# Holding back the first store, longer load rows, and a closing barrier moved to GpSimd, in a 2x nearest-neighbour upsampling kernel

## The chip, the cores and the metric

The kernel runs on one core of a Trainium2 chip. The metric is the device time of one execution in microseconds (us), as the median of several runs. From one run to the next the time of one kernel moves by 0.1 to 0.7 us, and the effects discussed here are of that order on about 199 us. So the times are always set beside the kernel before from the same rounds on the same chip, and the trace, which resolves nanoseconds, is used to tell where the time lies. The span of a trace (first to last instruction) is about 1.8 us shorter than the reported time.

## The reference

```python
x: (16, 64, 64, 64) float32, scale_factor = 2
result: (16, 64, 128, 128) float32
result[:, :, i, j] = x[:, :, i // 2, j // 2]
```

Every input value is written four times: 16.78 MB are read and 67.11 MB written, 83.89 MB in all. There is no arithmetic.

## The kernel before

The input is seen as 65536 rows of 64 numbers. It is loaded in four DMAs of 4 MB, all issued at the start on SyncE's queue into the 128 partitions. The first three put 32 KB of consecutive data into each partition; the fourth is cut into four bands, so that a partition gets four pieces of 8 KB. VectorE expands 9/16 of each chunk and ScalarE the rest into one of two buffers, and a DMA on the same SyncE queue stores the buffer: eight stores of 4 MB (one row of 32 KB per partition), then four of 8 MB (64 KB per partition).

```python
M4 = R // (4 * P)                       # 128 input rows per partition and block
blocks = [(1, M4, 0), (1, M4, 2), (1, M4, 3), (4, M4 // 4, 1)]
... # cut
for n, (j, m, slot) in enumerate(blocks):
    first = n * P * M4
    xt = mem[:, slot * WB : (slot + 1) * WB].rearrange("p (j m w) -> p j m w", j=j, m=m)
    nc.sync.dma_start(
        out=xt.rearrange("p j m w -> p j (m w)"),
        in_=xf[first : first + P * M4, :].rearrange("(j p m) w -> p j (m w)", j=j, p=P),
    )
... # cut
def store(part, r0, k, at):
    xp, first, m = part
    kv = k * 9 // 16
    u = mem[:, at : at + k * s * W * s].rearrange("p (k a w b) -> p k a w b", k=k, a=s, w=W)
    nc.vector.tensor_copy(out=u[:, :kv], in_=expanded(xp[:, r0 : r0 + kv, :]))
    nc.scalar.copy(out=u[:, kv:], in_=expanded(xp[:, r0 + kv : r0 + k, :]))
    dst = of[first : first + P * m, :].rearrange("(p m) w -> p m w", p=P)
    nc.sync.dma_start(out=dst[:, r0 : r0 + k, :], in_=u)

small = [(q, r0) for n in (0, 3) for q in parts[n] for r0 in range(0, q[2], 32)]
large = [(q, r0) for n in (1, 2) for q in parts[n] for r0 in range(0, q[2], 64)]
for n, (q, r0) in enumerate(small):
    store(q, r0, 32, WX + n % 2 * (WU // 2))
for n, (q, r0) in enumerate(large):
    store(q, r0, 64, (0, WX)[n % 2])
```

At the end of the program SyncE waits for all DMAs, then all five engines meet at a barrier, GpSimd clears the semaphores, and they meet at a second barrier.

Of the kernel before, what the change touches and what calls it, by code (L numbers as in the profile page):

```python
# [1 line left out]

# [4 lines left out]



EARLY = 1  # L10


def begin_before_barrier(nc):



    blocks = nc.main_func.blocks
    main, body = blocks[0], blocks[1]
    sp = mybir.EngineType.SP
    loads = [i for i in body.instructions if i.engine == sp][:EARLY]  # L20
    for load in loads:
        assert isinstance(load, mybir.InstDMACopy), type(load)
        assert not (load.sync_info and load.sync_info.on_wait)
    names = [i.name for i in loads]
    body.instructions = [i for i in body.instructions if i.name not in names]
    kept = list(main.instructions)
    at = next(
        n
        for n, i in enumerate(kept)
        if i.engine == sp and isinstance(i, mybir.InstDrain)  # L30
    )
    kept[at:at] = loads
    main.instructions = kept


@with_exitstack
def kernel(
    ctx: ExitStack,
    tc: tile.TileContext,
    x: bass.AP,  # L40
    scale_factor: int,
    out: bass.AP,
):
    nc = tc.nc
    nc.at_finalize(begin_before_barrier)
    P = nc.NUM_PARTITIONS
    s = int(scale_factor)
    B, C, H, W = x.shape
    R = B * C * H
    fdt = x.dtype  # L50



    WX = R // P * W
    WU = 16384
    mem_pool = ctx.enter_context(tc.tile_pool(name="mem", bufs=1))
    mem = mem_pool.tile([P, WX + WU], fdt, name="mem")



    M4 = R // (4 * P)
    blocks = [(1, M4, 0), (1, M4, 2), (1, M4, 3), (4, M4 // 4, 1)]
    WB = M4 * W
    assert M4 * P * 4 == R and 2 * WB == WU

    xf = x.rearrange("b c h w -> (b c h) w")
    of = out.rearrange("b c (h hd) w -> (b c h) (hd w)", hd=s)

    parts = []
    for n, (j, m, slot) in enumerate(blocks):  # L70
        first = n * P * M4
        xt = mem[:, slot * WB : (slot + 1) * WB].rearrange(
            "p (j m w) -> p j m w", j=j, m=m
        )
        nc.sync.dma_start(
            out=xt.rearrange("p j m w -> p j (m w)"),
            in_=xf[first : first + P * M4, :].rearrange(
                "(j p m) w -> p j (m w)", j=j, p=P
            ),
        )  # L80
        parts.append([(xt[:, jj], first + jj * P * m, m) for jj in range(j)])

    def expanded(rows):
        return rows.unsqueeze(2).unsqueeze(4).to_broadcast(
            [P, rows.shape[1], s, W, s]
# [6 lines that stand above are left out]
        u = mem[:, at : at + k * s * W * s].rearrange(  # L92
            "p (k a w b) -> p k a w b", k=k, a=s, w=W
        )
        nc.vector.tensor_copy(out=u[:, :kv], in_=expanded(xp[:, r0 : r0 + kv, :]))  # L95
        nc.scalar.copy(out=u[:, kv:], in_=expanded(xp[:, r0 + kv : r0 + k, :]))  # L96
        dst = of[first : first + P * m, :].rearrange("(p m) w -> p m w", p=P)
        nc.sync.dma_start(out=dst[:, r0 : r0 + k, :], in_=u)



    small = [(q, r0) for n in (0, 3) for q in parts[n] for r0 in range(0, q[2], 32)]
    large = [(q, r0) for n in (1, 2) for q in parts[n] for r0 in range(0, q[2], 64)]
    for n, (q, r0) in enumerate(small):
        store(q, r0, 32, WX + n % 2 * (WU // 2))
    for n, (q, r0) in enumerate(large):
        store(q, r0, 64, (0, WX)[n % 2])


# [1 line left out]
_INS = ['x', 'scale_factor']  # L111
_OUTS = [((16, 64, 128, 128), 'float32')]

_NUMBERS = {'scale_factor': 2}


# [26 lines left out]
```

## Time and profile before

| | before |
|---|---|
| time, median of the first 3 runs | 199.46 us (199.43 to 199.73) |
| span of the trace | 197.71 us |
| VectorE, ScalarE busy | 20%, 26% |
| DMA queue busy, mean rate over the span | 98.9%, 424 GB/s |
| last load landed / first store landed / last store landed | 42.19 / 51.90 / 196.90 us |
| last landing to end of span | 0.81 us |

These lines are from the page of the kernel before. The DMA row gives the busy share of the DMA engines in tenths for 40 slices of the span. The queue line gives packets, MB, and the share of the 16 engines' time. The last three lines give DMA groups: count, KB each, and the median time from issue to landing.

```profile
span 197.7 us, 116 instructions
DMA  8999999999999999999999999999999999999994
q1 hardware_dynamic: 2688, 83.89, 98.9%
HBM read 16.78 MB, written 67.11 MB: 424 GB/s over the span
out_dram<-mem SPq DMA_DIRECT2D x8, 4096.0 KB, 16.1
mem<-in_x_dram SPq DMA_DIRECT2D x4, 4096.0 KB, 25.8
out_dram<-mem SPq DMA_DIRECT2D x4, 32.3
```

The DMA engines are busy 90% or more in every slice but the first and the last. A store takes 16.1 us from issue to landing only because it waits about 6.4 us behind its predecessor; the pace itself has to be read from successive landings. The chain of waits shows it. Its columns are start, duration and what it was; a DMA piece runs from issue to landing. The part from 64 to 120 us:

```profile
64.87 16.05 DMA out_dram<-mem
80.92 0.02 issue
80.94 0.02 ACTq L96
80.95 0.04 issue
81.00 3.19 ACT mem L96
84.18 0.02 issue
84.20 16.08 DMA out_dram<-mem
100.28 0.02 issue
...
103.56 16.09 DMA out_dram<-mem
```

From 64.87 to 84.20 the chain makes one round, in which the queue moves two stores: 19.33 us, or 9.67 us for 4 MB, which is 434 GB/s. The next round is 19.36 us.

The waits of SyncE (SPq), which issues the DMAs (two lines of five; what waited, for what: us in total, times, longest), show when the first store can go and where the end is spent:

```profile
SPq L98 <- DVE mem L95: 143.5, 11, 35.7
SPq L138 <- DMA out_dram<-mem: 31.8, 2, 19.3
```

SyncE never waits for a load before it issues a store; it waits for the copies, VectorE's above all, and at the end (L138 is the end of the program) for the last stores.

### The profile page before, as it was taken

How to read it: one execution, taken by the hardware profiler on the slowest of the kernel's cores; microseconds unless marked ns; L12 is line 12 of the kernel's file. 1: busy time of each engine (PE TensorE's matmuls, PEld its weight loads, DVE VectorE, ACT ScalarE, POOL GpSimd, SP SyncE). 2: the span in 40 equal slices, each digit the busy share in tenths (PEclk: the TensorE clock that was granted, in tenths of full speed). 3: DMA queues.
4: the chain of work that ended last, by engine and by line, in shares of the span. 5: the costliest groups of instructions: out<-in, count | busy, mean ns of one | idle time of the engine just before them, and what ended most of it. 6: DMA issues, size and time to landing. Idle time of an engine off the chain costs nothing.

```text
span 197.7 us, 116 instructions
## 1 busy us (share of the span) xinstructions
DVE 40.2 (20%) x12; ACT 51.3 (26%) x13; POOL 0.2 (0%) x4
## 2 busy tenths in 40 slices
DVE  0055000000405059505050007200810090000000
ACT  2057000000415150606069207400830092000000
POOL 0000000000000000000000000000000000000000
DMA  8999999999999999999999999999999999999994
GB/s 318 424 424 424 438 464 383 424 413 424 424 424 424 444 444 451 451 424 438 424 424 424 424 424 424 464 477 491 451 451 424 424 424 424 424 424 424 424 424 212
DMA packets 2688, 83.89 MB, mean 424 GB/s; under 512 B 256, under 2 KB 256, under 8 KB 256
## 3 DMA queue, kind: packets, MB, share of 16 engines
q1 hardware_dynamic: 2688, 83.89, 98.9%
HBM read 16.78 MB, written 67.11 MB: 424 GB/s over the span
## 4 chain that ended last, share of the span: by engine, by line
DMA 69%; ACT 14%; issue 0%; ACTq 0%
DMA out_dram<-mem 63%; ACT mem L96 14%; DMA mem<-in_x_dram 6%; ACTq L96 0%
## 5 line engine op out<-in xcount | busy, mean ns | idle before, releaser
L96 ACT COPY mem<-mem 128x3584 f32<-128x3584 f32 (+1 forms) x12 | 50.0, 4174 | 112.5 <-DMA out_dram<-mem 102.2
L95 DVE COPY mem<-mem 128x4608 f32<-128x4608 f32 (+1 forms) x12 | 40.2, 3359 | 123.1 <-DMA out_dram<-mem 110.8
L96 ACT ACT_TABLE_LOAD x1 | 1.3, 1283 | 0.8 <-PEq L124 0.8
L124 POOL MEMSET const-bfloat16-1.0<- 128x1 bf16 x1 | 0.1, 102 | 0.0
L124 POOL MEMSET const-uint8-127<- 128x1 uint8 x1 | 0.1, 102 | 0.0
L124 POOL MEMSET const-float32-0.0<- 128x1 f32 x1 | 0.1, 99 | 0.2 <-issue 0.2
L124 POOL MEMSET const-float32-1.0<- 128x1 f32 x1 | 0.1, 99 | 0.0
## 6 DMA issues: line engine op xcount, KB each, us to landing
out_dram<-mem SPq DMA_DIRECT2D x8, 4096.0 KB, 16.1
mem<-in_x_dram SPq DMA_DIRECT2D x4, 4096.0 KB, 25.8
out_dram<-mem SPq DMA_DIRECT2D x4, 32.3
```

Source lines behind the costliest of these rows:

```text
L95: nc.vector.tensor_copy(out=u[:, :kv], in_=expanded(xp[:, r0 : r0 + kv, :]))
L96: nc.scalar.copy(out=u[:, kv:], in_=expanded(xp[:, r0 + kv : r0 + k, :]))
L124: nc = _bacc.Bacc("TRN2", target_bir_lowering=False, num_devices=1)
```

## The change

The intent: (1) the fourth load gets long rows like the others, cut into a part of 104 rows (26 KB per partition) and a last part of 24 rows (6 KB); (2) the first store is held until the 26 KB part has landed, so that stores begin as the loads end; (3) the closing is rearranged: both gatherings of the engines and the first release happen while the last stores are still under way, and GpSimd alone waits for the last landing, clears the semaphores and gives the last release.

```diff
+def close_on_gpsimd(nc):
+    ... # cut: finds the last store's semaphore and the closing instructions
+    waits = sorted(wait.sync_info.on_wait, key=lambda w: w.id != last)
+    d0, gather0, release0, d1, clear, d2, gather1, release1 = mine
+    landed = mybir.InstDrain(... engine=pool, sync_info=mybir.SyncInfo(on_wait=waits, on_update=[]))
+    others = [i for i in end if i.engine != pool and i is not wait]
+    blocks[-1].instructions = others + [
+        d0, gather0, release0, gather1, d1, landed, clear, d2, release1
+    ]
...
+    nc.at_finalize(close_on_gpsimd)
...
-    blocks = [(1, M4, 0), (1, M4, 2), (1, M4, 3), (4, M4 // 4, 1)]
+    slots = [0, 2, 3, 1]
+    TAIL = 24
...
+        cuts = (0, M4 - TAIL, M4) if n == len(slots) - 1 else (0, M4)
+        for lo, hi in zip(cuts, cuts[1:]):
+            loads.append(nc.sync.dma_start(out=xt[:, lo:hi], in_=src[:, lo:hi]))
...
     for n, (q, r0) in enumerate(small):
-        store(q, r0, 32, WX + n % 2 * (WU // 2))
+        st = store(q, r0, 32, WX + n % 2 * (WU // 2))
+        if n == 0:
+            tc.add_manual_dep(
+                st.ins,
+                loads[-2].ins.name,
+                mybir.DependencyInfo(
+                    mybir.DependencyClass.Sync, mybir.DependencyReason.DATA
+                ),
+                reason="stores begin as the loads end",
+            )
```

More of the change, by code (lines that the diff above doesn't have):

```diff
@@ L33, in begin_before_barrier @@
     main.instructions = kept
+def close_on_gpsimd(nc):
+    blocks = nc.main_func.blocks
+    sp, pool = mybir.EngineType.SP, mybir.EngineType.Pool
+    stores = [
+        i
+        for i in blocks[1].instructions
+        if i.engine == sp and isinstance(i, mybir.InstDMACopy)
+    ]
+    last = stores[-1].sync_info.on_update[0].id
+    end = list(blocks[-1].instructions)
+    wait = end[0]
+    assert wait.engine == sp and isinstance(wait, mybir.InstDrain)
+    waits = sorted(wait.sync_info.on_wait, key=lambda w: w.id != last)
+    assert waits[0].id == last and len(waits) > 2
+    mine = [i for i in end if i.engine == pool]
+    kinds = [type(i).__name__ for i in mine]
+    assert kinds == [
+        "InstDrain",
+        "InstEventSemaphore",
+        "InstEventSemaphore",
+        "InstDrain",
+        "InstISA",
+        "InstDrain",
+        "InstEventSemaphore",
+        "InstEventSemaphore",
+    ], kinds
+    d0, gather0, release0, d1, clear, d2, gather1, release1 = mine
+    landed = mybir.InstDrain(
+        name=wait.name,
+        engine=pool,
+        debug=wait.debug,
+        sync_info=mybir.SyncInfo(on_wait=waits, on_update=[]),
+    )
+    others = [i for i in end if i.engine != pool and i is not wait]
+    blocks[-1].instructions = others + [
+        d0, gather0, release0, gather1, d1, landed, clear, d2, release1
+    ]
 @with_exitstack
@@ L69 @@
     parts = []
-    for n, (j, m, slot) in enumerate(blocks):
+    loads = []
+    for n, slot in enumerate(slots):
         first = n * P * M4
-        xt = mem[:, slot * WB : (slot + 1) * WB].rearrange(
-            "p (j m w) -> p j m w", j=j, m=m
-        )
-        nc.sync.dma_start(
-            out=xt.rearrange("p j m w -> p j (m w)"),
-            in_=xf[first : first + P * M4, :].rearrange(
-                "(j p m) w -> p j (m w)", j=j, p=P
-            ),
-        )
-        parts.append([(xt[:, jj], first + jj * P * m, m) for jj in range(j)])
+        xt = mem[:, slot * WB : (slot + 1) * WB].rearrange("p (m w) -> p m w", m=M4)
+        src = xf[first : first + P * M4, :].rearrange("(p m) w -> p m w", p=P)
+        cuts = (0, M4 - TAIL, M4) if n == len(slots) - 1 else (0, M4)
+        for lo, hi in zip(cuts, cuts[1:]):
+            loads.append(nc.sync.dma_start(out=xt[:, lo:hi], in_=src[:, lo:hi]))
+        parts.append([(xt, first, M4)])
     def expanded(rows):
@@ L97, in store @@
         dst = of[first : first + P * m, :].rearrange("(p m) w -> p m w", p=P)
-        nc.sync.dma_start(out=dst[:, r0 : r0 + k, :], in_=u)
+        return nc.sync.dma_start(out=dst[:, r0 : r0 + k, :], in_=u)
     small = [(q, r0) for n in (0, 3) for q in parts[n] for r0 in range(0, q[2], 32)]
@@ L104 @@
     for n, (q, r0) in enumerate(small):
-        store(q, r0, 32, WX + n % 2 * (WU // 2))
+        st = store(q, r0, 32, WX + n % 2 * (WU // 2))
[7 more added lines that the diff above has]
+                reason="stores begin as the loads end",
+            )
     for n, (q, r0) in enumerate(large):
```

## The prediction

> **What bounds the kernel.** The DMA queue. On the page the DMA row reads 9 in nearly every slice, one queue takes 98.9% of the span, and 83.89 MB move at a mean 424 GB/s; VectorE and ScalarE are 20% and 26% busy. Landings in the trace are evenly spaced: 9.65 to 9.71 us for every 4 MB DMA with 32 KB rows, 19.3 us for 8 MB with 64 KB rows: 434 GB/s, loads and stores alike.[...] Only what lies around the stream can go.
>
> Loads and stores share one queue, in order: the first store is issued at 15.5 us but lands at 51.9, 9.71 us after the last load (42.19). So they mix only at the handover.
>
> **What is not stream in the span** (DMA packet records, landings): [...]10.54 us for the fourth load instead of 9.71, so 0.83 too much; 0.80 us from the last landing (196.90) to the span's end. Of the 0.83: its 8 KB packets take 309 ns against 1213/4 = 303, over 32 packets per engine about 0.15 us with some slower ones. The other 0.68 us is in the last three or four 8 KB packets of each engine (400 to 900 ns each), just where the store packets follow.[...]
>
> **The change, costed.**
> 1. Load rows of 26 and 6 KB instead of 8 KB: saves about 0.13 us.
> 2. Hold: the first store is issued when the 26 KB part has landed; 6 KB per partition is left, 8 packets per engine, about 1.85 us (estimate: 48 KB at 27 bytes/ns). Landing notice 0.4 us, wake and issue 0.1, issue to first packet 1.0 to 1.5 (first load of the trace): the engines should just run dry, for 0.1 to 0.2 us[...]. The last loads are no longer slowed. Net: 0.25 us gained, between 0.5 lost and 0.7 gained. The copies have slack (store 3 issued at 55.2, store 2 in flight until 61.6).
> 3. Closing: before, after the last landing SyncE passes a wait and two drains, GpSimd gathers and releases, all drain, GpSimd clears, gathers and releases again. After, both gathers and the first release are done early; GpSimd's wait, clear (93 ns), drain and release remain. The intervals in the trace add up to 0.42 us instead of 0.80: 0.38 saved, all critical.
>
> **Prediction.** 199.46 − 0.13 − 0.25 − 0.38 = 198.7 us; 198.2 to 199.3 should hold it 8 times in 10. Faster by over 2%: 0.005; within 2%: 0.985; slower by over 2%: 0.01.
>
> **What would show it.** (a) Last landing to end of span falls from 0.80 to about 0.42 us. (b) The last load lands about 41.4 instead of 42.2. (c) First store issued near 40.2, landing near 51.4 to 51.6. (d) Later landings still every 9.7 and 19.3 us.
>
> **What would make it wrong.** A DMA issue slower to start than 1.5 us once warm, a visible gap at 41 us; or the 0.68 us belonging to the handover itself[...] and reappearing in the first store: then 198.95 to 199.4. Or the reported time not following the span at its end, so that the closing's 0.38 us stays unseen.

Passages that no trace or run of this case shows are cut from the recorded text and marked. The sum came to 198.7 us: 0.13 for the rows, 0.25 for the hold and 0.38 for the closing taken from 199.46. The inputs of the hold's estimate are from the trace of the kernel before: 27 bytes/ns is a 32 KB packet in 1213 ns; from an engine's last packet (with its completion) to the landing pass 0.34 to 0.40 us, mean of each DMA; the first 16 packets of the first load start 1.01 to 1.56 us after its issue. What slows the last loads at the handover was not shown, and that only what lies around the stream can go was my estimate.

## The result, and the profile after

The changed kernel takes 198.98 us (198.82 to 199.19, 6 runs) against 199.56 us of the kernel before (6 runs): ratio 0.9972, 95% interval 0.9959 to 0.9985. A ratio here is the mean time of one kernel's fast runs over that of the other's of the same rounds, so it is not quite the ratio of the medians quoted. The change is a real gain of about 0.3%, inside the predicted range.

Lines of the same page, after (its DMA row is that of before, digit for digit):

```profile
span 197.4 us, 117 instructions
q1 hardware_dynamic: 2448, 83.89, 98.9%
out_dram<-mem SPq DMA_DIRECT2D x8, 4096.0 KB, 16.2
mem<-in_x_dram SPq DMA_DIRECT2D x3, 4096.0 KB, 21.4
mem<-in_x_dram SPq DMA_DIRECT2D x1, 3328.0 KB, 38.1
mem<-in_x_dram SPq DMA_DIRECT2D x1, 768.0 KB, 39.4
out_dram<-mem SPq DMA_DIRECT2D x4, 32.4
```

The stores, which the change does not touch, take 0.1 us longer from issue to landing: 16.2 for 16.1 and 32.4 for 32.3. The chain of waits after has the same part of the execution as this:

```profile
1.66 38.12 DMA mem<-in_x_dram
39.77 0.02 issue
39.79 0.03 SPq L142
39.82 0.05 issue
39.86 0.35 SPq L142
...
64.42 16.19 DMA out_dram<-mem
80.60 0.02 issue
...
83.89 16.19 DMA out_dram<-mem
...
103.35 16.23 DMA out_dram<-mem
```

The first lines are the hold: the first store is issued at 39.86 us, just after the 26 KB part has landed. Below, a round of two stores now takes 83.89 - 64.42 = 19.47 us instead of 19.33. The kernel after is 0.45 us ahead at 64 us (64.42 for 64.87), 0.31 ahead at 84 us, and 0.21 ahead at 103 us (103.35 for 103.56). It gives its lead back store by store. SyncE's waits after (two lines of five):

```profile
SPq L142 <- DMA mem<-in_x_dram: 37.1, 1, 37.1
SPq L192 <- PEq L192: 32.2, 2, 32.0
```

The first line is the hold. In the second, SyncE's wait for the last stores has become a wait in the closing barrier. The view puts it down to TensorE's queue (PEq), which waits at the same barrier; in the trace GpSimd's release at 197.309 us comes just before SyncE goes on at 197.351. In instruction starts (us) from the two traces, the end of the program is:

```
before  last landing 196.899; SyncE wait 196.916, drains 196.981 and 197.039;
        GpSimd gather 197.071, release 197.149, drain 197.230, clear 197.329,
        drain 197.451, gather 197.529, release 197.607; last engine done 197.712
after   last landing 197.037; GpSimd wait 197.061, clear 197.124, drain 197.246,
        release 197.309; last engine done 197.414
```

So 0.81 us have become 0.38. The table follows the landings of whole DMAs (the last of the 16 engines) through both traces, with a second trace of the kernel after:

| us | before | after | after, again |
|---|---|---|---|
| last load landed | 42.19 | 41.63 | 41.52 |
| first store landed | 51.90 | 51.39 | 51.21 |
| last store landed | 196.90 | 197.04 | 196.72 |
| from first to last store | 145.00 | 145.64 | 145.50 |
| last landing to end of span | 0.81 | 0.38 | 0.38 |
| span | 197.71 | 197.41 | 197.09 |

The hold wins 0.5 to 0.7 us by the first store, and the eleven stores after it lose 0.5 to 0.6 us. The closing's 0.44 us is most of what remains. The loss is in the single packets. There is one packet per row and partition (1024 of 32 KB for the eight stores of 4 MB, 512 of 64 KB for the four of 8 MB, shared by 16 engines); this is their duration in the trace's DMA records:

```
ns per store packet        32 KB (55 to 115 us)      64 KB (after 120 us)
before                     1213, none longer          2418, none longer
after                      mean 1219.7, 1213 to 1244  mean 2423.9, up to 2446
after, again               mean 1219.3, up to 1246    mean 2423.8, up to 2446
```

Before, store packets follow each other like a clock. After, they are uneven and some 6 ns longer. After the landing of the first store an engine still moves 56 packets of 32 KB and 32 of 64 KB: 56 x 6.5 + 32 x 5.9 ns = 0.55 us, which is the loss. Below, a packet is called flat when it takes just the 1213 or 2418 ns of the kernel before.

### The profile page after: what moved, and what is told of

It is laid out like the page before. It is cut to its first block, busy times and chain, and to the rows that moved or that the text cites. A ratio compares the mean times of both kernels' runs of the same rounds, so it can differ in the third digit from the quotient of the medians.

```text
span 197.4 us, 117 instructions
## 1 busy us (share of the span) xinstructions
DVE 40.2 (20%) x12; ACT 51.3 (26%) x13; POOL 0.2 (0%) x4
## 2 busy tenths in 40 slices
DMA packets 2448, 83.89 MB, mean 425 GB/s; under 512 B 272, under 2 KB 272, under 8 KB 400
## 3 DMA queue, kind: packets, MB, share of 16 engines
q1 hardware_dynamic: 2448, 83.89, 98.9%
## 4 chain that ended last, share of the span: by engine, by line
DMA 71%; ACT 11%; SPq 1%; issue 0%; ACTq 0%
DMA out_dram<-mem 52%; DMA mem<-in_x_dram 19%; ACT mem L140 11%; SPq L124 0%; SPq L142 0%; ACTq L140 0%
## 6 DMA issues: line engine op xcount, KB each, us to landing
out_dram<-mem SPq DMA_DIRECT2D x8, 4096.0 KB, 16.2
out_dram<-mem SPq DMA_DIRECT2D x4, 32.4
```

## The experiments

Three theories were in play. Theory A: the engines keep the flat pace as long as the queue has the next packet ready, and the hold lets it run dry at the handover, after which the pace is the uneven one. Rival B: the uneven packets come from the split load, the closing or the chip of that run. Later, within A, two forms: C, the stores gain a lead at the handover that is used up packet by packet, so nothing is really won or lost; and D, the pace is set at the handover and stays. These were guesses to be tested; how a lead would come about inside the DMA engines was not shown.

In all tables, landings are means over the 16 engines unless said otherwise, and "dry" is the mean time between the end of an engine's last load packet (with its completion) and the start of the first store packet, from the DMA records; -3 ns is the usual overlap of neighbouring packets.

### One part at a time

`no_hold`: the kernel after without the hold.

```diff
-        if n == 0:
+        if False:
```

> The changed kernel without the hold; 26 KB and 6 KB load rows and the GpSimd closing stay. Theory A ([...]the hold empties it, and then every store packet costs a few ns more): the 32 KB store packets take 1213 ns flat again instead of 1219.5, landings of stores are 9.68 us apart instead of 9.74, the last load lands near 42.0, the first store near 51.8, last landing to end 0.38 us, and the time is 198.7 to 198.9 us, as fast as the changed kernel or a little faster. Rival B (the longer packets come from the split load, the closing or the chip of that run): packets stay at 1218 to 1220 ns, and the time is about 199.3 us, because the hold's gain at the handover is lost.

`c_only`: the kernel before with the closing alone.

```diff
+def close_on_gpsimd(nc): ... # as in the change
+    nc.at_finalize(close_on_gpsimd)
```

> The kernel before with only the GpSimd closing. Last landing to end of span 0.38 us instead of 0.81; time 0.43 us under the kernel before, 199.1 us, if the reported time follows the span at its end. Under A store packets stay at 1213 ns. Under B by way of the closing they lengthen to 1219 ns, and the gain is gone.

`r_only`: the kernel before with the fourth load in rows of 32 KB, unsplit.

```diff
-    blocks = [(1, M4, 0), (1, M4, 2), (1, M4, 3), (4, M4 // 4, 1)]
+    blocks = [(1, M4, 0), (1, M4, 2), (1, M4, 3), (1, M4, 1)]
```

> The kernel before with only one load row of 32 KB per partition in the fourth load (no split, no hold, old closing). The fourth load lands 0.12 to 0.16 us earlier (42.05 instead of 42.19); its last 32 KB packet of each engine is about 0.7 us longer than 1213 ns[...]; store packets 1213 ns under A; time 199.4 us, 0.13 under the kernel before. If small rows had caused the slow packets at the handover, the fourth load would land at 41.4 and the time would be 198.8 us.

`after_again`: the kernel after, unchanged.

> The changed kernel again, as control beside the others. Under A its store packets are again uneven and 1218 to 1220 ns on the mean for 32 KB and 2422 to 2424 for 64 KB; if that trace was a chance of its chip, they are 1213 and 2418. Time 198.9 to 199.1 us.

Measured, on one chip, where the kernel before took 199.42 us (9 runs); each has 5 runs:

| | time us | ratio to before (95%) | last load | first to last store | packets ns | last landing to end |
|---|---|---|---|---|---|---|
| before (first trace) | | | 41.88 | 145.03 | 1213 / 2418 | 0.81 |
| `no_hold` | 199.24 | 0.9993 (0.9981 to 1.0006) | 42.20 | 145.05 | 1213 / 2418 | 0.38 |
| `c_only` | 199.13 | 0.9986 (0.9973 to 0.9998) | 41.84 | 145.03 | 1213 / 2418 | 0.38 |
| `r_only` | 199.67 | 1.0014 (1.0002 to 1.0027) | 41.89 | 145.03 | 1213 / 2418 | 0.81 |
| `after_again` | 198.89 | 0.9979 (0.9965 to 0.9992) | 41.18 | 145.57 | 1219 / 2424 | 0.38 |

Rival B falls: with the split load and the new closing but no hold, the packets are flat, and with the hold they are uneven again in a second trace. The uneven pace belongs to the hold.

The closing is worth 0.44 us in the trace and 0.29 us in the medians (199.13 for 199.42; the interval of the ratio runs from 0.04 to 0.54 us, so the two agree). Nothing of it is lost elsewhere: `c_only`'s landings are those of before to within 0.05 us.

The longer rows are worth nothing. In `r_only` the fourth load lands 10.54 us after the third (last engine), exactly as in the kernel before. Its last 32 KB packets take up to 2.02 us instead of 1.21, so the delay at the handover is there with long rows too, and the 309 ns for 303 of an 8 KB packet do not show in the landing. The median is even 0.25 us above before; the trace of its fastest run (199.48 us) does not show why the other four were slower, and this stays open.

`no_hold` brought a surprise: with the split into 26 and 6 KB and no hold, the last load lands 0.32 us later than before, and some 6 KB packets take 1.13 us. The split alone makes the handover worse; my 198.7 to 198.9 us for this run was too low, in the main for that reason. Hold and split can only be judged together: from `c_only` to `after_again` they bring 0.24 us in the medians and 0.16 in the means. The intervals of the two ratios overlap, so with 24 rows their gain is not shown clear of noise.

### How much must be left in the queue when the store is issued?

If running dry is the cause, the cure is a longer last part, so that the store is issued earlier. `tail26`, `tail28`, `tail32`, `tail36`, `tail42` and `tail16` change one number of the kernel after:

```diff
-    TAIL = 24
+    TAIL = 26   # 28, 32, 36, 42, 16
```

> The changed kernel with a last load part of 26 rows (6.5 KB) instead of 24, so that the first store comes about 0.15 us earlier against the end of the loads. Theory A: a short overlap[...] is all that the steady rate needs, so a part or all of the engines' packets go back to 1213 ns while the last load is delayed by about 0.15 us: time 198.6 to 198.9 us. If only a completely filled queue holds the rate, packets stay at 1219 ns and the time is that of the changed kernel plus 0 to 0.15.

> 28 rows (7 KB): the first store about 0.3 us earlier than in the changed kernel. Theory A: last load delayed by about 0.3 us (mean landing 41.5 instead of 41.2), all store packets at 1213 and 2418 ns, landings of stores 9.68 and 19.31 us apart, which saves 0.5 to 0.6 us over the store phase; time 198.6 to 198.7 us, 0.2 to 0.3 under the changed kernel. Rival: packets at 1219 ns whatever the tail until the overlap is complete, and then the time is 199.2.

> 32 rows (8 KB): the first store about 0.6 us earlier. Theory A: last load delayed by 0.6 us, store packets 1213 ns; time about 198.9 to 199.0, more than with 28 rows: the overlap beyond what is needed is paid for once and brings nothing.

> 16 rows (4 KB): the first store about 0.6 us later than in the changed kernel. Both theories: the engines run dry at the handover for 0.6 us, seen as a gap between the last load packet and the first store packet of every engine; store packets at 1219 ns as in the changed kernel; time 199.4 to 199.6 us.

> 36 rows (9 KB) in the last load part. The runs with 26, 28 and 32 rows did not fill any lead; this one goes on towards the unheld order. Theory C: a lead[...] is a stock. It costs what the last loads are delayed, and 6 to 7 ns of it are used up with every store packet[...]. So if the lead comes out partial, the store packets are 1213 ns flat until it is used up and then uneven at 1219 ns, and the mean landing of the last store stays at 196.4 to 196.6 whatever the handover costs; time 198.8 to 198.9 us. Theory D: once full, the lead holds for good and packets stay at 1213 ns to the end, with time 198.5 us or less for a partial lead.

> 42 rows (10.5 KB): store packets are on the queue before the reads of the loads end, so the lead should be nearly complete: last load delayed by 0.6 to 0.8 us against the changed kernel, store packets 1213 and 2418 ns to the end or nearly so, mean landing of the last store 196.5 to 196.6; time 198.9 to 199.15 us under theory C, that of the closing alone.

The kernel before took 199.46 us in the rounds of 16 to 32 rows and 199.49 us in those of 36 and 42, on two chips. The row for 24 is `after_again`.

| rows in the last part | time us | ratio (95%) | store issued | dry, ns | last load | first to last store | 32 KB packet, mean ns | last store |
|---|---|---|---|---|---|---|---|---|
| 24 | 198.89 | 0.9979 (0.9965 to 0.9992) | 39.75 | 73 | 41.18 | 145.57 | 1219.3 | 196.48 |
| 26 | 198.96 | 0.9977 (0.9964 to 0.9989) | 39.49 | 55 | 41.14 | 145.55 | 1219.5 | 196.42 |
| 28 | 198.91 | 0.9972 (0.9960 to 0.9985) | 39.43 | 53 | 41.17 | 145.55 | 1219.5 | 196.44 |
| 32 | 198.81 | 0.9965 (0.9951 to 0.9979) | 39.05 | 37 | 41.18 | 145.53 | 1219.3 | 196.42 |
| 36 | 198.67 | 0.9954 (0.9941 to 0.9967) | 38.82 | 15 | 41.23 | 145.16 | 1215.3 | 196.09 |
| 42 | 198.29 | 0.9940 (0.9927 to 0.9952) | 38.37 | -3 | 41.21 | 144.94 | 1213.1 | 195.84 |
| (16: not held) | 198.97 | 0.9974 (0.9962 to 0.9987) | 18.62 | -3 | 41.91 | 145.05 | 1213.0 | 196.65 |

Up to 32 rows my expectations missed: I had thought that the store's first packet comes 0.9 to 1.0 us after its issue and that 28 rows would already give an overlap. In `after_again` the first store packet came 0.86 us after the issue (39.75 to 40.60 us). With 32 rows, where more load packets were still in the queue, the first store packets of the engines came at 40.75 us on the mean, 1.7 us after the issue at 39.05 us, and the last load packets were done at 40.72 us. The dry time fell only slowly (the first trace of the kernel after has 154 ns), the packets stayed at 1219 ns, and the last load was not delayed.

With 36 rows the dry time is 15 ns on the mean and two thirds of the store packets are flat. In that run the spread between the first and the last engine's landing grows from 0.60 us at the first store to 1.05 us at the last, which fits engines that keep different paces. The records do not name the engine, but at the handover ends and starts can be paired: 13 engines go on with the usual overlap of 3 or 4 ns, and three pause, for 93 ns on the mean. Of the packets that come second on the 16 engines, twelve are flat and four take 1244 to 1254 ns; and from 48 to 80 us 76% of all packets are flat, as if twelve engines of 16 were, later 62 to 74%. So the pace goes by engine, and the pause accounts for three of the four. With 32 rows eight engines pause, and eight of the second packets take 1242 to 1255 ns; but the other engines lose the flat pace within the next tens of us. In these runs, not to run dry at the handover was thus needed but not enough: the flat pace was kept to the end on all engines only by a still earlier issue (38.37 us with 42 rows, below), and where between 36 and 42 rows the bound lies was not measured.

With 42 rows no engine runs dry, 96% or more of the packets are flat in every slice from 46 us to the end, and the last load still lands as early as with 24 rows, where I had expected it 0.6 to 0.8 us later and 198.9 to 199.15 us in all. The chain of waits of `tail42` shows both gains at once:

```profile
1.64 36.64 DMA mem<-in_x_dram
...
64.17 16.04 DMA out_dram<-mem
80.21 0.02 issue
...
83.50 16.03 DMA out_dram<-mem
...
102.81 16.07 DMA out_dram<-mem
```

The round from 64.17 to 83.50 is 19.33 us again, as before the change, and it starts 0.70 us earlier than in the kernel before (64.87). This version, 198.29 us, is faster than both kernels: 0.6% under before, twice the gain of the change as it was made.

`tail16` did not test what it was meant to. With 16 rows the scheduler put the second store ahead of the held one in SyncE's order, so that a store was issued at 18.62 us and the queue was never dry. It serves as a further unheld run: flat packets, and a last load that lands 0.7 us later than with the hold.

### Is it the hold, or the dry queue? And does the pace last?

`gap`: the kernel before, no hold, but the fifth store waits until the fourth has landed.

```diff
+        if n == 3:
+            fourth = st
+        if n == 4:
+            tc.add_manual_dep(st.ins, fourth.ins.name, ...,
+                reason="let the queue run dry once")
```

> The kernel before, with the fifth store issued only when the fourth has landed (about 80.9 us), so that the queue runs dry once in the middle; no hold at the start. The stores before it: packets of 1213 ns flat. After it: uneven and 1219 ns for 32 KB and 2424 for 64 KB, under C and D alike, since the lead is lost. The gap itself is about 1.3 us[...]; C says the time rises by 1.3 us less about 0.2. If packets stay at 1213 ns after the gap, a dry queue is not what makes them uneven, and both theories fall.

`rows16k`: the kernel before with each store cut into DMAs of 16 rows, so 256 store packets of 16 KB per engine instead of 96.

```diff
-        nc.sync.dma_start(out=dst[:, r0 : r0 + k, :], in_=u)
+        for c in range(0, k, 16):
+            nc.sync.dma_start(
+                out=dst[:, r0 + c : r0 + c + 16, :], in_=u[:, c : c + 16]
+            )
```

> The kernel before with every store cut into DMAs of 16 rows, so 16 KB per packet and 256 store packets per engine instead of 96. Theory C: the lead of about 0.83 us from the handover lasts for some 130 packets at 6 to 7 ns each; packets are flat (about 609 ns) in the first half of the store phase and uneven and longer (614 to 617 ns) in the second, and the time rises by about 1 us over the kernel before. Theory D: flat to the end; only the fixed few ns of more packets are added, some 0.6 to 0.9 us.

Against 199.49 us of before, `gap` took 201.35 us (4 runs, ratio 1.0091, 95% 1.0078 to 1.0104) and `rows16k` 200.81 us (4 runs, 1.0063, 1.0050 to 1.0076). The chain of waits of `gap`:

```profile
64.72 16.07 DMA out_dram<-mem
80.78 0.02 issue
...
84.06 17.64 DMA out_dram<-mem
101.71 0.02 issue
...
104.99 16.23 DMA out_dram<-mem
```

The piece of 17.64 us contains the gap. Before it the store packets are 1213 ns in all records. From 86 us to the end of the 32 KB stores they are uneven, with means of 1216 to 1220 ns in slices of 8 us, and the 64 KB packets are 2421 to 2430. The later piece of 16.23 us is that of the kernel after, not that of before. So a dry queue in the middle of the stores, without any hold, has the same effect, and it lasts to the end: 110 us later the packets are still uneven. The time fits: the fifth store lands 11.21 us after the fourth instead of 9.69, which is 1.52 us, and the uneven pace adds some 0.4 us; the measured difference is 1.86 us. So nothing comes off for a lead that is saved at the end, as theory C wanted.

In `rows16k`, 99% or more of the packets are 611 ns in every slice up to the end; its last store lands 1.0 us later than before (mean 197.60 for 196.61) with 160 more packets per engine. Packets of 1213 and 2418 ns leave 8 ns that do not grow with the size (2 x 1213 - 2418), 5 after the usual overlap of 3 ns, so by this estimate 160 packets add 0.8 us. A lead used up at 6.5 ns a packet would have cost 256 x 6.5 = 1.66 us, twice the 0.83 us by which the fourth load was delayed in the kernel before. Theory C falls here, and once more in `tail42`, which paid nothing at the handover and still kept the flat pace. Theory D comes nearest: a queue that passes the handover without running dry keeps the flat pace to the end (in all seven such traces), and one that runs dry does not find it again (64 KB packets of 2424 ns in `after_again`, 2421 to 2430 in `gap`). It has to be softened at the edge: with 32 rows a third of the packets were still flat at 55 us and 13% at 105 us, so where there is hardly any lead the flat pace is lost on the way, as the engines that did not pause show. What inside the DMA engines makes the two paces is not settled by these runs.

Two things stay open. One is why stores that have been queued long before (at 15 to 19 us) delay the last loads by 0.7 to 1.0 us (mean landing 41.88 in the kernel before and 42.20 in `no_hold`, for 41.18 in `after_again`), while one queued 2.8 us before the last landing does not (41.21 in `tail42`). The delay lies in the last load packets, up to 898 ns for 8 KB in the kernel before where the median is 309; its cause was not shown. The other is where between 42 rows and the unheld order that delay comes back; 42 is the largest that was tried.

## Why the prediction was right or wrong

The total was right: 198.98 us measured against 198.7 predicted, range 198.2 to 199.3, and "within 2%" at 0.985. Of the forecast gain of 0.76 us (from 199.46), 0.58 came (from 199.56). Point by point:

- What bounds the kernel: right. The stream fills the span in all traces, and only fractions of a us around it moved.
- The closing, "0.38 saved, all critical": right. The trace shows 0.44 us; by itself it gave 0.29 us in the medians.
- "Load rows of 26 and 6 KB instead of 8 KB: saves about 0.13 us": wrong. Long rows alone saved nothing (fourth load 10.54 us after the third in both), and split without hold they cost 0.32 us at the handover. I had added up packet durations, which did not add to the landing.
- The hold, "Net: 0.25 us gained": the sum came near by cancellation, which is luck, and even its sign is not shown clear of noise. "The last loads are no longer slowed" was right and larger than counted: the last load lands 0.70 us earlier (mean landing 41.18 for 41.88). "The engines should just run dry" was right too. The cost of running dry was mis-sized: I counted the dry time itself, 0.1 to 0.2 us, measured at 0.07 to 0.15, and not what follows it.
- Check (d), "Later landings still every 9.7 and 19.3 us", failed, and it is the step that went wrong: the steady rate of the stores was taken as a given that a pause cannot change. Landings came 9.74 and 19.36 us apart (9.68 and 19.31 before), 0.5 to 0.6 us over the store phase. Rows and hold together brought 0.16 to 0.24 us instead of 0.38.
- The doubt "the 0.68 us belonging to the handover itself and reappearing in the first store" did not come true: the first store landed 0.5 to 0.7 us earlier.

## What to carry to other kernels

Where a DMA queue is saturated, look at the durations of single packets, not only at the busy share: 98.9% before and 98.9% after hid a change of 0.4% in pace. A pause of a few tens of ns in the queue can cost more than its own length (here 73 ns on the mean went with 0.54 us over the store phase, 145.57 for 145.03), so a transfer that is meant to start "just as the last one ends" should be issued early enough that the queue does not run dry in any engine, with some lead to spare (with 36 rows 13 engines of 16 did not pause, and a third of the packets were still not flat), and the margin found by trying (here 42 rows instead of 24). Judge a change of three parts by its parts: here one part carried most of the gain, one was worth nothing, and one brought little that is clear of noise until a number chosen too small was raised.
